# A different beginning: c broadcast by DMA, the first sums on TensorE, and another order of loads and modulation in a two-layer encoder

## The chip, the cores and the metric

The kernel runs on one core of a Trainium2 chip. The metric is the device time of one execution in microseconds, the median of several runs; lower is better. The core has TensorE (PE, with its weight loads listed apart as PEld), VectorE (DVE), ScalarE (ACT), GpSimd (POOL) and SyncE (SP), which issues the transfers between HBM and SBUF. All engines work through queues of their own and wait for one another by semaphores.

## The reference

The reference is an encoder trunk with two layers over 256 tokens of width 2048, in float32. Only the first steps matter for this change; the rest is given in words.

```python
c_act = jax.nn.silu(c)
for l in range(DEPTH):
    mod = c_act @ ada_w[l] + ada_b[l]
    sh_a, sc_a, gt_a, sh_m, sc_m, gt_m = [t[:, None, :] for t in jnp.split(mod, 6, axis=-1)]
    h = rmsnorm(x, norm_mix[l]) * (1.0 + sc_a) + sh_a
    qa, ka, va, qb, kb, vb, ga, gb = split_cols(h @ w_in[l])
    ...  # two attentions, two gates, projections, x = x + gt_a * (merged @ w_out[l])
    h = rmsnorm(x, norm_ffn[l]) * (1.0 + sc_m) + sh_m
    ...  # gated MLP with a convolution over positions, x = x + gt_m * (... @ w_down[l])
```

So the first product `h @ w_in` needs three things: the mean square of each token of x, the shift and scale of each of the 16 chunks of 128 channels (from c and `ada_w`), and the weights.

## The kernel before

**Layout.** Channels lie on the 128 partitions: x is 16 chunks (KC) of 128 channels by 256 tokens. Each weight element is used once for all 256 tokens, so all weights pass through SBUF once, in the order in which they are used.

**Weights.** They come as units of 16 blocks of 128 by 128, one transfer of 1024 KB each (`unit`, L231). ScalarE rounds a unit to a high half (L240), VectorE takes the difference as the low half (L241), and each block then costs three matmuls: high times high, high times low, low times high. In the form `tokens` (L325 to L327), used for q, k and v, four blocks make six matmuls of 512 columns, three for each half of the tokens; in the form `features` (L249 to L251) a block makes three matmuls of 256 columns.

**Modulation.** `ada(l)` makes the 96 columns of shift, scale and gate of a layer. Each column group takes one tile of `ada_w`, 1024 KB, which VectorE multiplies by silu(c) and sums along the free dimension (L172). That wants silu(c) on every partition, in `cact`. The order is shift and scale of chunk 0, then of chunk 1, and so on. Weight tiles and modulation tiles share one pool of four buffers, `raw`.

**The beginning, in program order.** c is loaded as one row of 8 KB (L140); four matmuls with a column of ones copy it to all partitions, and ScalarE applies silu to each quarter (L145, L146). x comes in four transfers of 512 KB (L545). ScalarE squares each quarter of x (L551), VectorE adds the quarters (L553) and folds the four chunks that are left to one (L555), and two matmuls with a column of 1/2048 give each token's mean square (L558, L559). GpSimd raises it to -1/2 (L386), TensorE transposes it to a row (L392), six matmuls on the identity follow as warm-up (L341), and ScalarE copies the row to SBUF (L397). Then h of each chunk is made in three steps: VectorE (L405), ScalarE (L408) and VectorE (L409).

**Parts of q, k and v.** In layer 0 the product with `w_in` is cut along the 16 input chunks into four parts of 2, 4, 5 and 5 chunks (`K_PARTS_0`), so that it can begin before all modulation is there. Each part runs nine column groups of q, k and v and then the 16 groups of gate A over its chunks, and adds to the sums of the parts before (L678 copies in part 0, L680 adds later; L709 and L712 for the gate). A part's blocks make 6.5, 13, 16.25 and 16.25 units.

**Pacing.** `job0` makes modulation and h for one chunk after another. Before part 0 it is run until 4 tiles (2 chunks) are done. It then runs in the background: at the end of each unit `bg.tick()` adds `FIRST_RATE` (0.65) to a count, and for every whole number one tile is made. At the start of a later part, `while done[0] < 2 * (part[-1] + 1)` makes whatever is still missing for that part: 12 tiles in all for part 1, 22 for part 2, 32 for part 3.

**Small tables.** `small(l)` loads the attention mask, the rotary tables, gains, sinks and convolution weights, and forms the rotary tables with gains on VectorE (L572, L577). It is called after the first column group of part 0. Its results are first used in the last part.

**Order.** The framework plans the order of each engine's queue at build time: by the order of the program as priority, and by when it expects an operation's inputs to be there. So an engine's queue can differ from program order, but once built it is worked strictly in its order.

Of the kernel before, what the change touches and what calls it, by code (L numbers as in the profile page):

```python
# [9 lines left out]
F32 = mybir.dt.float32  # L10
F32R = mybir.dt.float32r
AF = mybir.ActivationFunctionType
ALU = mybir.AluOpType
AX = mybir.AxisListType

P = 128
L = 2
D = 2048
S = 256
KC = D // P  # L20
# [6 lines left out]
EPS = 1e-6  # L27
# [18 lines left out]
ADA_PLAN_0 = [(38, 32), (58, 48), (76, 66), (84, 70), (96, 80), (128, 96), (145, 108), (175, 118), (192, 124), (230, 143)]  # L46
ADA_PLAN_1 = [(0, 143), (76, 169), (84, 165), (95, 176), (129, 192)]

FIRST_RATE = 0.65
ENDING = 15  # L50
FIRST = 0

WARM = [1, 4, 3]
WARM_IN = 6
AHEAD = 2
HELD = 2
LATE = 3
# [48 lines left out]
def encoder(ctx: ExitStack, tc: tile.TileContext, a: dict, out: bass.AP):  # L106
    nc = tc.nc
# [3 lines left out]
    def skip(n, p=None):  # L111

        skips.append((p or pool(f"skip{len(skips)}", 1)).tile([P, n // 4], F32, name=f"skip{len(skips)}"))
        nc.vector.memset(skips[-1][:], 0.0)
# [9 lines left out]
    sm = pool("sm", 3)  # L124
    mm = pool("mm", 4, space=bass.MemoryType.PSUM)
    ax = pool("ax", 3, space=bass.MemoryType.PSUM)
# [3 lines left out]
    mean = const.tile([P, 1], F32, name="mean")  # L130
# [6 lines left out]
        return t  # L137

    cact = const.tile([P, D], F32, name="cact")
    nc.sync.dma_start(cact[:1], a["c"])  # L140
    one = sm.tile([1, P], F32, name="one", tag="one", bufs=1)
    nc.vector.memset(one[:], 1.0)
    for i in range(0, D, 512):
        cb = ax.tile([P, 512], F32, name="cb", tag="ax")
        nc.tensor.matmul(cb[:], one[:], cact[:1, i : i + 512], start=True, stop=True)  # L145
        nc.scalar.activation(out=cact[:, i : i + 512], in_=cb[:], func=AF.Silu)  # L146
    x = const.tile([P, KC, S], F32, name="x")
    skip(96, const)
    skip(64)
    sp = pool("s", 1)  # L150

    def place(tag, n, dt, name):
        return sp.tile([P, n, S], dt, name=name, tag=tag)
# [6 lines left out]
    mods, amods, nrms, done = {}, {}, {}, {0: 0, 1: 0}  # L160
# [63 lines left out]
    bg = Paced()  # L224
# [111 lines left out]
    def warm(n):  # L336

        if n:
            ps = ax.tile([P, 512], F32, name="warm", tag="ax")
            for _ in range(n):  # L340
                tc.keep_in_program_order(nc.tensor.matmul(ps[:, :P], ident[:], ident[:], start=True, stop=True))  # L341
# [33 lines left out]
    def normed(l, w, sums, st, first=False):  # L375
# [3 lines left out]
        def steps():  # L379
# [10 lines left out]
            for t in range(2):  # L390
                tc.keep_in_program_order(
                    nc.tensor.transpose(rb[:, t * P : (t + 1) * P], rs[:, t : t + 1].broadcast_to([P, P]), ident[:])  # L392
                )
            warm(WARM_IN if first else WARM[2])
            if first:
# [108 lines left out]
    def urgent(yes):  # L504
        return tc.high_priority() if yes else nullcontext()
# [7 lines left out]
    def ada_all():  # L513
        yield from gens[0]
        yield from gens[1]

    adas = ada_all()
# [14 lines left out]
    def ada_and_h(steps):  # L532

        for kc in range(KC):
            while done[0] < 2 * kc + 1:
                next(adas)
                yield
            next(adas)
            next(steps)
            yield  # L540

    for _ in range(FIRST):
        next(adas)
    for i in range(0, KC, 4):
        nc.sync.dma_start(x[:, i : i + 4], a["xT"][:, i : i + 4])  # L545

    mean_sq = sm.tile([P, 2], F32, name="ms_in", tag="nsa")
    acc = place("y0", 4, F32, "sq_in")
    for i in range(0, KC, 4):
        sq = acc if i == 0 else place(f"y{1 + i // 4 % 2}", 4, F32, f"sq_in{i}")  # L550
        nc.scalar.activation(out=sq[:], in_=x[:, i : i + 4], func=AF.Square)  # L551
        if i:
            nc.vector.tensor_tensor(out=acc[:], in0=acc[:], in1=sq[:], op=ALU.add)  # L553
    for n in (2, 1):
        nc.vector.tensor_tensor(out=acc[:, :n], in0=acc[:, :n], in1=acc[:, n : 2 * n], op=ALU.add)  # L555
    ps = ax.tile([P, 2], F32, name="ss_in", tag="ss", bufs=1)
    for t in range(2):
        nc.tensor.matmul(ps[:, t : t + 1], acc[:, 0, t * P : (t + 1) * P], mean[:], start=True, stop=True)  # L558
    nc.vector.tensor_scalar(out=mean_sq[:], in0=ps[:], scalar1=EPS, scalar2=None, op0=ALU.add)  # L559

    tables = []

    def small(l):

        if l == 0:
            tables.extend((load(a["maskA"], [P, 2, S], "maskA"), load(a["cs"], [P, 2, 2, HALF], "cs")))
        cs = tables[1]
        gains = load(a["gains"][l], [P, 4], f"gains{l}", lay, tag="gains")
        rg = load(a["rg"][l], [P, 2, ROT], f"rg{l}", lay, tag="rg")
        sink = load(a["sink"][l], [P, HA], f"sink{l}", lay, tag="sink")  # L570
        cw = load(a["cw"][l], [P, 2 * FC, 4], f"cw{l}", lay, tag="cw", bufs=1)
        nc.vector.tensor_scalar(out=gains[:, 2:3], in0=gains[:, 2:3], scalar1=SCALE, scalar2=None, op0=ALU.mult)  # L572
        rots = []
        for w in range(2):
            rot = lay.tile([P, 4, 2, HALF], F32, name=f"rot{l}_{w}", tag=f"rot{w}")
            for i, (f, g) in enumerate(((0, 0), (1, 1), (0, 1), (1, 0))):
                nc.vector.tensor_tensor(  # L577
                    out=rot[:, i], in0=cs[:, f],
                    in1=rg[:, w, g * HALF : (g + 1) * HALF].unsqueeze(1).broadcast_to([P, 2, HALF]), op=ALU.mult,
                )  # L580
            rots.append(rot)

        return gains, sink, cw, rots

    for l in range(L):
        st = Stream(l) if l == 0 else nxt
        h, steps = normed(l, 0, None if l == 0 else sums, st, first=l == 0)
        mod = mods.get(l)
        if l == 0:
            job0 = ada_and_h(steps)  # L590
            while done[0] < 2 * len(K_PARTS[0][0]):
                next(job0)
            mod = mods[0]
            bg.add(job0, FIRST_RATE)
        else:
            with urgent(True):
                for _ in range(FEED):
                    next(steps)
            st.steps, st.fed = steps, FEED
# [63 lines left out]
        parts = K_PARTS[l]  # L663
        for pi, part in enumerate(parts):
            if l == 0 and pi > 0:
                while done[0] < 2 * (part[-1] + 1):
                    next(job0)
            last = pi == len(parts) - 1
            for g in range(len(QKV_GROUPS)):
                pss = st.tokens(h, part)  # L670
                if pi == 0 and g == 0:
                    gains, sink, cw, rots = small(l)
                dst = packs[g // 3][:, 4 * (g % 3) : 4 * (g % 3) + 4]
                rows = dst.rearrange("p (t a) s -> p t (a s)", t=2)
                if not last or pi > 0:
                    for t, ps in enumerate(pss):
                        if pi == 0:
                            nc.scalar.copy(rows[:, t], ps[:])  # L678
                        else:
                            nc.vector.tensor_tensor(out=rows[:, t], in0=ps[:], in1=rows[:, t], op=ALU.add)  # L680
                    pss = [rows[:, t] for t in range(2)]
                if not last:
                    continue

                def have(g=g):
                    ready[0] = g + 1

                vcol = {0: GA * HEAD, 4: 0, 7: 0}.get(g)
                if vcol is not None and pi == 0:
                    for t in range(2):  # L690
                        nc.scalar.copy(rows[:, t, vcol:], pss[t][:, vcol:])
                if g == 0:
                    qk_rows(pss, GA, rots[1], gains[:, 1:2], kTa, have)
                elif g < 3:
                    qk_rows(pss, 4, rots[0], gains[:, 0:1], dst, have)
                elif vcol is None:
                    qk_rows(pss, 4, None, gains[:, 3:4] if g in (3, 6) else gains[:, 2:3], dst, have)
                else:
                    have()
                if g == 2:  # L700
                    bg.add(job, ATT[l])


            for mo in range(KC):

                def gate_a(ps):
                    src = ps
                    if pi > 0:
                        nc.vector.tensor_tensor(out=ya[:, mo], in0=ps, in1=ya[:, mo], op=ALU.add)  # L709
                        src = ya[:, mo]  # L710
                    if last:
                        nc.scalar.activation(out=ya[:, mo], in_=src, func=AF.Sigmoid)  # L712
                    elif pi == 0:
                        nc.scalar.copy(ya[:, mo], ps)

                st.features([hs[k] for k in part], [gate_a])
# [11 lines left out]
        for tag in ("y0", "y1", "y2"):  # L728
            t = place(tag, 4, F32, f"gb{l}_{tag}")
            gb += [t[:, i] for i in range(4)]  # L730
        for i in range(2):
            t = ev.tile([P, 2, S], F32, name=f"gb{l}_{i}", tag="u", bufs=2)
# [38 lines left out]
        for mos in OUT_TURNS:  # L771
            end = mos[0] == KC - 1
            if end:
                st.prefetch(AHEAD + 1)
            with urgent(mos[0] >= ENDING):
# [18 lines left out]
        for gi, chunks in enumerate(FF_GROUPS):  # L794
# [48 lines left out]
            for mos in OUT_TURNS:  # L843
                end = mos[0] == KC - 1
                ending = last and mos[0] >= ENDING
                if last and end and l < L - 1:
                    nxt = Stream(l + 1)
                    nxt.prefetch(AHEAD)
                with urgent(ending):
# [76 lines left out]
```

## Time and profile before

| what | value |
|---|---|
| median of 3 runs | 2740.95 us (2740.84 to 2763.34) |
| profiled execution | 2756.37 us |
| its span | 2754.6 us |
| PE busy | 2697.4 us, 98% |
| VectorE busy | 2077.5 us, 75% |
| ScalarE busy | 1371.3 us, 50% |
| read from HBM | 695.03 MB, 253 GB/s over the span |
| modulation tiles, weight units | 192 and 464 transfers of 1024 KB |

How to read it: TensorE's time is nearly the whole span, so an engine's idle time matters only where TensorE waits for it. The profile's slices are 69 us long and coarse; the beginning is read from windows of 2 to 20 us and from the timeline. "PEclk" is the clock that TensorE was granted, as a share of full speed. A matmul's listed duration contains its way through the pipeline, so the pace is read from counts or from the distance between starts, not from durations. A row that ends in "x6" gathers six instructions.

### The profile page before, as it was taken

To read this page: it belongs to the slowest core of one execution; us is meant where nothing else is said; L and a number is where in the kernel's file an instruction comes from. 1 tells how busy PE (TensorE), PEld (TensorE's weight loads), DVE (VectorE), ACT (ScalarE), POOL (GpSimd) and SP (SyncE) were. 2 spreads that over 40 slices of the span, in tenths; PEclk is the share of its full clock that TensorE was granted. 3 is DMA by queue.
4 is the path that set the end of the run, shared out by engine and by line. 5 is a ranking of instruction groups with operands and counts; after the bars stand their busy time and mean duration, and the time that the engine had idled before them with its cause. 6 is when DMAs were issued, how large, how long until landed. Compare 5 with 4: busy or idle time off the path is not lost.

```text
span 2754.6 us, 49972 instructions
## 1 busy us (share of the span) xinstructions
PE 2697.4 (98%) x21136; PEld 2601.5 (94%) x21136; DVE 2077.5 (75%) x2814; ACT 1371.3 (50%) x1897; POOL 39.3 (1%) x24
## 2 busy tenths in 40 slices
PE   7899999999999999999999999999999999999999
PEld 5788799998999999999988889999999999999999
DVE  6998987998887777678877665657888856665664
ACT  5344784444553455345444557544455535544553
POOL 0000100000000000000000000000000000000000
PEclk9999999999999999999999999999999999999999
DMA  8887588986778766677756556665858755555554
GB/s 317 334 333 262 219 303 326 349 337 242 275 283 316 277 248 252 253 277 284 280 197 258 220 211 247 234 249 203 294 221 301 264 192 191 199 192 191 199 188 149
DMA packets 101890, 700.36 MB, mean 254 GB/s; under 512 B 12705, under 2 KB 15009, under 8 KB 17697
## 3 DMA queue, kind: packets, MB, share of 16 engines
q1 hardware_dynamic: 101666, 697.17, 68.5%
q8 instruction: 165, 2.70, 0.4%
q14 instruction: 59, 0.48, 0.0%
HBM read 695.03 MB, written 2.10 MB: 253 GB/s over the span
## 4 chain that ended last, share of the span: by engine, by line
PE 73%; issue 15%; DVE 6%; DMA 2%; ACT 2%; POOL 1%; POOLq 0%; SPq 0%; ACTq 0%; DVEq 0%
PE ps L251 20%; PE ps L249 20%; PE ps L250 20%; PE ps_t L326 4%; PE ps_t L327 4%; PE ps_t L325 4%; DVE hl L241 2%; DVE aw L172 2%; DMA aw<-in_aw 1%; DMA w<-in_ws 1%; POOL qrs L373 1%; ACT hl L240 1%; PE sc L468 1%; PE po L499 1%; DVE qn L432 0%
## 5 line engine op out<-in xcount | busy, mean ns | idle before, releaser
L241 DVE TENSOR_TENSOR hl<-w,hl 128x1024 fp32r<-128x1024 f32 x928 | 1130.6, 1223 | 401.4 <-ACT hl L240 400.0
L240 ACT CAST hl<-w 128x1024 fp32r<-128x1024 f32 x928 | 971.1, 1049 | 850.8 <-PE ps L251 578.9
L249 PE MATMUL ps<-h,hl 128*128 128x256 f32 x3840 | 1073.8, 280 | 3.3 <-ACT hl L240 2.0
L251 PE MATMUL ps<-h,hl 128*128 128x256 f32 x3840 | 1073.6, 280 | 0.0
L250 PE MATMUL ps<-h,hl 128*128 128x256 f32 x3840 | 1072.7, 279 | 0.0
L250 PEld LDWEIGHTS ps<-h,hl 128*128 128x128 f32 x3840 | 728.8, 190 | 0.4
L249 PEld LDWEIGHTS ps<-h,hl 128*128 128x128 f32 x3840 | 723.9, 189 | 4.4 <-ACT hl L240 2.2
L251 PEld LDWEIGHTS ps<-h,hl 128*128 128x128 f32 x3840 | 722.9, 188 | 0.3 <-DVE hl L241 0.2
L172 DVE CUSTOM_DVE_ANT_0 aw<-aw,cact,ab 128x2048 f32<-128x2048 f32 x192 | 450.7, 2347 | 48.5 <-DMA aw<-in_aw 47.7
L790 DVE SCALAR_TENSOR_TENSOR u<-ps,cw,u 128x255 f32<-128x255 f32 x352 | 168.3, 482 | 104.0 <-ACT u L788 97.7
L325 PE MATMUL ps_t<-hl,h 128*128 128x512 f32 x576 | 227.9, 400 | 7.9 <-ACT hl L240 7.2
L326 PE MATMUL ps_t<-hl,h 128*128 128x512 f32 x576 | 228.5, 397 | 4.7 <-DVE hl L241 4.7
L327 PE MATMUL ps_t<-hl,h 128*128 128x512 f32 x576 | 227.5, 396 | 0.9 <-DVE h L409 0.9
L788 ACT ACTIVATE u<-ps,cw 128x256 f32<-128x256 f32 x176 | 98.7, 565 | 247.6 <-PE ps L251 247.6
L250 PE MATMUL ps<-merged,hl 128*128 128x256 f32 x512 | 144.3, 282 | 0.0
L249 PE MATMUL ps<-merged,hl 128*128 128x256 f32 x512 | 143.9, 282 | 0.3 <-DVE m L749 0.3
L251 PE MATMUL ps<-merged,hl 128*128 128x256 f32 x512 | 144.1, 281 | 0.0
L250 PE MATMUL ps<-act_o,hl 128*128 128x256 f32 x512 | 142.9, 279 | 0.0
L251 PE MATMUL ps<-act_o,hl 128*128 128x256 f32 x512 | 142.8, 279 | 0.0
L249 PE MATMUL ps<-act_o,hl 128*128 128x256 f32 x512 | 142.5, 279 | 0.0
L325 PEld LDWEIGHTS ps_t<-hl,h 128*128 128x128 f32 x576 | 109.6, 191 | 31.9 <-ACT hl L240 8.3
L326 PEld LDWEIGHTS ps_t<-hl,h 128*128 128x128 f32 x576 | 109.8, 191 | 30.4 <-DVE hl L241 8.1
(162 smaller groups left out, 3755.8 us busy)
## 6 DMA issues: line engine op xcount, KB each, us to landing
w<-in_ws SPq DMA_DIRECT2D x464, 1024.0 KB, 4.9
aw<-in_aw SPq DMA_DIRECT2D x192, 1024.0 KB, 5.0
bias<-in_bias SPq DMA_DIRECT2D x16, 256.0 KB, 5.1
x<-in_xT SPq DMA_DIRECT2D x4, 512.0 KB, 5.2
out<-x SPq DMA_DIRECT2D x16, 128.0 KB, 2.8
cw<-in_cw SPq DMA_DIRECT2D x2, 176.0 KB, 5.5
maskA<-in_maskA SPq DMA_DIRECT2D x1, 256.0 KB, 5.3
ab<-in_ab SPq DMA_DIRECT2D x2, 48.0 KB, 5.9
```

The costliest lines, as they stand in the source:

```text
L172: nc.vector.tensor_tensor_reduce(out=raw[:], in0=raw[:], in1=cact[:], scale=1.0, scalar=ab[:, i : i + 1], op0=ALU.mult, op1=ALU.add, accum ...
L240: nc.scalar.copy(hl[:, 0], r)
L241: nc.vector.tensor_tensor(out=hl[:, 1], in0=r, in1=hl[:, 0].bitcast(F32), op=ALU.subtract)
L249: nc.tensor.matmul(out, hi, act[:, 0], start=first, stop=False)
L250: nc.tensor.matmul(out, hi, act[:, 1], start=False, stop=False)
L251: nc.tensor.matmul(out, lo, act[:, 0], start=False, stop=last)
L325: nc.tensor.matmul(ps[:], xh, hi, start=kc == kcs[0], stop=False)
L326: nc.tensor.matmul(ps[:], xh, lo, start=False, stop=False)
L327: nc.tensor.matmul(ps[:], xl, hi, start=False, stop=kc == kcs[-1])
L373: nc.gpsimd.tensor_tensor(out=dst, in0=src, in1=mhalf[:, :k], op=ALU.pow)
L788: nc.scalar.activation(out=u, in_=ps, func=AF.Identity, scale=w[:, 1:2], bias=w[:, 3:4])
L790: nc.vector.scalar_tensor_tensor(out=u[:, to], in0=ps[:, of], scalar=w[:, j : j + 1], in1=u[:, to], op0=ALU.mult, op1=ALU.add)
```

## The change

Five edits, all in the beginning.

1. c is loaded straight to all 128 partitions by one transfer from a repeated row; the column of ones and its four matmuls go. Silu runs on two halves in SBUF. The transfers of x are issued right behind it.
2. The sums of squares: the quarters of x are squared by ScalarE and VectorE in turn, and TensorE sums all 16 chunks directly, with 32 one-column matmuls into two accumulators, kept in program order. VectorE adds epsilon to each. Fourteen warm-up matmuls follow.
3. `st.prefetch(1)` asks for the first weight unit after two modulation tiles, no longer after four.
4. The rate of `job0` is 1.25 tiles a unit in part 0, 0.8 in part 1 and 0.65 after that, no longer 0.65 throughout.
5. `small(l)` is called in the last part but one (part 2 in layer 0; in layer 1, which has one part, nothing changes).

```diff
-FIRST_RATE = 0.65
+FIRST_RATE = [1.25, 0.8, 0.65]
...
-FIRST = 0
...
+WARM_FIRST = 14
...
     cact = const.tile([P, D], F32, name="cact")
-    nc.sync.dma_start(cact[:1], a["c"])
-    one = sm.tile([1, P], F32, name="one", tag="one", bufs=1)
-    nc.vector.memset(one[:], 1.0)
-    for i in range(0, D, 512):
-        cb = ax.tile([P, 512], F32, name="cb", tag="ax")
-        nc.tensor.matmul(cb[:], one[:], cact[:1, i : i + 512], start=True, stop=True)
-        nc.scalar.activation(out=cact[:, i : i + 512], in_=cb[:], func=AF.Silu)
     x = const.tile([P, KC, S], F32, name="x")
+    nc.sync.dma_start(cact[:], a["c"].broadcast_to([P, D]))
+    for i in range(0, KC, 4):
+        nc.sync.dma_start(x[:, i : i + 4], a["xT"][:, i : i + 4])
+    for i in range(0, D, D // 2):
+        nc.scalar.activation(out=cact[:, i : i + D // 2], in_=cact[:, i : i + D // 2], func=AF.Silu)
...
-    acc = place("y0", 4, F32, "sq_in")
-    for i in range(0, KC, 4):
-        sq = acc if i == 0 else place(f"y{1 + i // 4 % 2}", 4, F32, f"sq_in{i}")
-        nc.scalar.activation(out=sq[:], in_=x[:, i : i + 4], func=AF.Square)
-        if i:
-            nc.vector.tensor_tensor(out=acc[:], in0=acc[:], in1=sq[:], op=ALU.add)
-    for n in (2, 1):
-        nc.vector.tensor_tensor(out=acc[:, :n], in0=acc[:, :n], in1=acc[:, n : 2 * n], op=ALU.add)
-    ps = ax.tile([P, 2], F32, name="ss_in", tag="ss", bufs=1)
+    ps = [ax.tile([P, 512], F32, name=f"ss_in{t}", tag="ax") for t in range(2)]
+    for i in range(0, KC, 4):
+        sq = place(f"y{i // 4 % 3}", 4, F32, f"sq_in{i}")
+        if i // 4 % 2:
+            nc.vector.tensor_tensor(out=sq[:], in0=x[:, i : i + 4], in1=x[:, i : i + 4], op=ALU.mult)
+        else:
+            nc.scalar.activation(out=sq[:], in_=x[:, i : i + 4], func=AF.Square)
+        for k in range(4):
+            for t in range(2):
+                tc.keep_in_program_order(
+                    nc.tensor.matmul(
+                        ps[t][:, :1], sq[:, k, t * P : (t + 1) * P], mean[:], start=i + k == 0, stop=i + k == KC - 1
+                    )
+                )
     for t in range(2):
-        nc.tensor.matmul(ps[:, t : t + 1], acc[:, 0, t * P : (t + 1) * P], mean[:], start=True, stop=True)
-    nc.vector.tensor_scalar(out=mean_sq[:], in0=ps[:], scalar1=EPS, scalar2=None, op0=ALU.add)
+        nc.vector.tensor_scalar(out=mean_sq[:, t : t + 1], in0=ps[t][:, :1], scalar1=EPS, scalar2=None, op0=ALU.add)
+    warm(WARM_FIRST)
...
             job0 = ada_and_h(steps)
+            while done[0] < 2:
+                next(job0)
+            st.prefetch(1)
             while done[0] < 2 * len(K_PARTS[0][0]):
                 next(job0)
             mod = mods[0]
-            bg.add(job0, FIRST_RATE)
+            bg.add(job0, FIRST_RATE[0])
...
                 while done[0] < 2 * (part[-1] + 1):
                     next(job0)
+                bg.pace(job0, FIRST_RATE[min(pi, len(FIRST_RATE) - 1)])
...
-                if pi == 0 and g == 0:
+                if pi == max(0, len(parts) - 2) and g == 0:
                     gains, sink, cw, rots = small(l)
```

More of the change, by code (lines that the diff above doesn't have):

```diff
@@ L540, in ada_and_h @@
             yield
-    for _ in range(FIRST):
-        next(adas)
+    mean_sq = sm.tile([P, 2], F32, name="ms_in", tag="nsa")
+    ps = [ax.tile([P, 512], F32, name=f"ss_in{t}", tag="ax") for t in range(2)]
     for i in range(0, KC, 4):
-        nc.sync.dma_start(x[:, i : i + 4], a["xT"][:, i : i + 4])
-    mean_sq = sm.tile([P, 2], F32, name="ms_in", tag="nsa")
-    acc = place("y0", 4, F32, "sq_in")
-    for i in range(0, KC, 4):
-        sq = acc if i == 0 else place(f"y{1 + i // 4 % 2}", 4, F32, f"sq_in{i}")
-        nc.scalar.activation(out=sq[:], in_=x[:, i : i + 4], func=AF.Square)
-        if i:
-            nc.vector.tensor_tensor(out=acc[:], in0=acc[:], in1=sq[:], op=ALU.add)
-    for n in (2, 1):
-        nc.vector.tensor_tensor(out=acc[:, :n], in0=acc[:, :n], in1=acc[:, n : 2 * n], op=ALU.add)
-    ps = ax.tile([P, 2], F32, name="ss_in", tag="ss", bufs=1)
+        sq = place(f"y{i // 4 % 3}", 4, F32, f"sq_in{i}")
[10 more added lines that the diff above has]
+                )
     for t in range(2):
-        nc.tensor.matmul(ps[:, t : t + 1], acc[:, 0, t * P : (t + 1) * P], mean[:], start=True, stop=True)
-    nc.vector.tensor_scalar(out=mean_sq[:], in0=ps[:], scalar1=EPS, scalar2=None, op0=ALU.add)
+        nc.vector.tensor_scalar(out=mean_sq[:, t : t + 1], in0=ps[t][:, :1], scalar1=EPS, scalar2=None, op0=ALU.add)
+    warm(WARM_FIRST)
     tables = []
```

## The prediction

> **What bounds the kernel now.** I read the page from the top: busy times, then the slices of the span.
>
> ```profile
> span 2754.6 us, 49972 instructions
> PE 2697.4 (98%) x21136; PEld 2601.5 (94%) x21136; DVE 2077.5 (75%) x2814; ACT 1371.3 (50%) x1897; POOL 39.3 (1%) x24
> ...
> PE   7899999999999999999999999999999999999999
> ...
> PEclk9999999999999999999999999999999999999999
> DMA  8887588986778766677756556665858755555554
> ```
>
> TensorE is busy 98% of the span, so what can be won is its idle time (57 us in all) and time at a lowered clock. The two slices below 9 are the first two, 69 us each, which is where the change works. Next I cut the beginning into windows; each row gives the stretch and its length, busy time (and instruction count) of PE, PEld, DVE, ACT, POOL, then granted clock, DMA share and GB/s.
>
> ```profile
> 0.00:10.00 10.00, 7.32 (x8) 2.32 (x8) 0.77 (x7) 6.14 (x7) 0.70 (x6) 1.00 0.80 283
> 10.00:20.00 10.00, 1.22 (x5) 0.93 (x4) 8.82 (x10) 2.49 (x3) 0.00 (x0) 1.00 0.97 395
> 20.00:30.00 10.00, 5.25 (x18) 4.25 (x19) 8.22 (x13) 3.26 (x5) 2.87 (x1) 1.00 0.99 370
> 30.00:40.00 10.00, 10.00 (x35) 7.97 (x35) 6.17 (x14) 4.95 (x8) 0.00 (x0) 1.00 0.55 202
> 40.00:60.00 20.00, 20.00 (x102) 16.59 (x101) 14.35 (x15) 15.86 (x26) 0.00 (x0) 1.00 0.82 310
> 60.00:80.00 20.00, 11.52 (x82) 9.85 (x81) 19.03 (x22) 8.84 (x20) 0.00 (x0) 0.81 0.97 353
> ...
> 100.00:120.00 20.00, 20.00 (x90) 16.54 (x90) 19.95 (x24) 9.16 (x10) 0.00 (x0) 1.00 0.89 334
> ...
> 200.00:240.00 40.00, 40.00 (x280) 37.40 (x279) 35.59 (x48) 16.25 (x17) 0.00 (x0) 1.00 0.85 311
> ...
> 440.00:480.00 40.00, 40.00 (x355) 40.00 (x354) 33.18 (x32) 15.63 (x21) 0.00 (x0) 1.00 0.93 347
> ```
>
> Three things stand here. From 10 to 30 us the DMA engines are full and TensorE does little: data is late. From 30 to 60 us the DMA share falls to 0.55 and 0.82 and VectorE is idle 3.8 + 5.65 = 9.5 us. From 60 to 80 us VectorE and DMA are full again while TensorE stands still 8.5 us. Work that could have been done between 30 and 60 is done too late. The counts also give the pace: 0.222 us for a 512-column matmul (100 to 120 us) and 0.113 us for a 256-column one (40 us / 355).
>
> The timeline shows what the stall is: a row is start, duration, engine, line, tile and, in brackets, the wait.
>
> ```profile
> 55.16 14.15 SPq L171 DMA_DIRECT2D aw<-in_aw  x6
> ...
> 64.14 2.35 DVE L172 CUSTOM_DVE_ANT_0 aw<-aw,cact,ab 128x2048 f32<-128x2048 f32 x1
> ...
> 78.18 2.35 DVE L172 CUSTOM_DVE_ANT_0 aw<-aw,cact,ab 128x2048 f32<-128x2048 f32 x1
> ...
> 79.79 1.22 PE L325 MATMUL ps_t<-hl,h 128*128 128x512 f32 x2 [6.89 <-ACT hl L240]
> 82.12 0.80 PE L326 MATMUL ps_t<-hl,h 128*128 128x512 f32 x1 [1.11 <-DVE hl L241]
> ```
> ```profile
> 74.00:76.00 2.00, 0.00 (x0) 0.00 (x0) 2.00 (x4) 0.00 (x0) 0.00 (x0) 0.50 1.08 385
> ...
> 84.00:86.00 2.00, 2.00 (x6) 1.62 (x5) 1.96 (x3) 1.08 (x2) 0.00 (x0) 0.50 0.93 303
> 86.00:88.00 2.00, 2.00 (x9) 1.58 (x9) 1.57 (x5) 1.00 (x2) 0.00 (x0) 0.95 0.96 406
> ```
>
> This is the border between part 0 (chunks 0 and 1) and part 1 (chunks 2 to 5). Part 0 is 104 blocks, 6.5 units of 16, and six units end in it. At 0.65 a unit that makes 3 modulation tiles on top of the first 4, so 12 - 7 = 5 are fetched and reduced at once. Some ten 512-column matmuls of part 1 get through before TensorE waits. It runs steadily from 82.1, and the clock is 0.50 until about 86, costing 2 us. Part 1 starts in effect at 82.1 - 10 x 0.222 + 2 = 81.9 us. That is the number to beat.
>
> **The change part by part.** First the prices: the beginning, then rows of the page.
>
> ```profile
> 2.63 7.58 PE L145 MATMUL cb<-cact,one 1*128 1x512 f32 x8 [2.63 <-DMA cact<-in_c]
> ...
> 9.54 1.23 DVE L553 TENSOR_TENSOR sq_in<-sq_in,sq_in 128x1024 f32<-128x1024 f32 x1 [8.41 <-ACT sq_in L551]
> ...
> 10.73 1.99 ACT L551 ACTIVATE sq_in<-x 128x1024 f32<-128x1024 f32 x2
> ...
> 17.75 0.93 PEld L558 LDWEIGHTS ss_in<-mean,sq_in 128*128 128x128 f32 x4 [9.13 <-DVE sq_in L555]
> ...
> 17.76 0.43 SPq L136 DMA_DIRECT2D maskA<-in_maskA  x1
> ...
> 20.13 2.87 POOL L386 TENSOR_TENSOR nrs<-ms_in,mhalf 128x2 f32<-128x2 f32 x1 [18.82 <-DVE ms_in L559]
> ...
> 20.37 0.43 SPq L136 DMA_DIRECT2D cw<-in_cw  x1
> ...
> 23.32 2.68 PEld L341 LDWEIGHTS warm<-ident 128*128 128x128 f32 x12
> ...
> 28.98 0.48 DVE L409 SCALAR_TENSOR_TENSOR h<-ht,mod,h 128x256 fp32r<-128x256 f32 x1
> 29.11 0.79 PE L326 MATMUL ps_t<-hl,h 128*128 128x512 f32 x1 [1.70 <-DVE hl L241]
> ...
> 30.64 0.90 DVE L577 TENSOR_TENSOR rot<-cs,rg 128x32 f32<-128x32 f32 x8
> ```
> ```profile
> L241 DVE TENSOR_TENSOR hl<-w,hl 128x1024 fp32r<-128x1024 f32 x928 | 1130.6, 1223 | 401.4 <-ACT hl L240 400.0
> ...
> L172 DVE CUSTOM_DVE_ANT_0 aw<-aw,cact,ab 128x2048 f32<-128x2048 f32 x192 | 450.7, 2347 | 48.5 <-DMA aw<-in_aw 47.7
> ...
> w<-in_ws SPq DMA_DIRECT2D x464, 1024.0 KB, 4.9
> aw<-in_aw SPq DMA_DIRECT2D x192, 1024.0 KB, 5.0
> ...
> maskA<-in_maskA SPq DMA_DIRECT2D x1, 256.0 KB, 5.3
> ```
>
> *c by DMA.* Gone are eight matmul passes (7.6 us) that lay beside the loading of x; they cost nothing. Added is a transfer that writes 128 rows of 8 KB, 1024 KB, ahead of x on a full queue: at 395 GB/s 1.049 MB is 2.65 us. No row shows a transfer that reads one row 128 times. Between nothing (if the repeated row is cheap) and twice that (5.3 us, if it is dear) I take 2.65, the price of the 1024 KB tiles nearest to it.
>
> *Weights sooner, small tables later.* Before, what must land for the first unit is x (2.1 MB), four modulation tiles and w0: 7.3 MB. After, the order is c, x, aw0, aw1, w0, aw2, aw3. The rows move 2.83 + 3.95 + 3.70 MB in the first 30 us, so 6.3 MB (w0) are through at 18.8 and 8.4 MB (aw3) at 24.3. There are four buffers, so aw3 is asked for only when aw0 has been reduced, around 16 to 17 us; that is in time. About 1 us of completion, 2.35 for its reduction and 1.4 for h of chunk 1 give 29.1; before, that h is written at 28.98 + 0.48. So chunk 0's six matmuls come earlier, chunk 1's do not: 0 to 2 us won.
>
> *Sums on TensorE.* VectorE loses three adds of 1.23 and two small ones and gets two products and two small ones: 2.2 us less. TensorE gets 16 x 2 matmuls, each two passes as in the row of ss_in (4 records for 2): 64 passes. At 0.93 us for four overlapping loads, and 2.68 for twelve, a pass takes 0.21 to 0.22 us, so 13.7 us; at double clock half of that. They start after both halves of silu and the first square, near 9.6, and end between 16.6 and 23.3. The end was 18.8 before. Fourteen warm-up matmuls (28 passes, 3 to 6 us) follow, beside the 2.87 us on GpSimd, and the transposes of the scale queue behind them. At half clock h of chunk 0 comes at about 31.4, at full clock the weights of 18.8 us set it.
> The cb row bears on which clock: eight passes of 512 columns in 7.6 us, with one row in use, hold the same 0.85 us a pass from first to last. The Trainium skill (TensorE: Matmul & The Clock Gate, Part 1: The HAM clock gate) says that some 3.4 us of sustained activity release the full clock; the cb row does not agree for thin matmuls. By the page the sums would take about 9 us and end near 18.5, by the row 13.7 us and 23.3.
>
> *More modulation in part 0.* At 1.25 a unit six units make 7 tiles, and one is left for the border instead of five. Each unit then needs 2.25 MB blocks. At 353 to 395 GB/s that is 6.0 to 6.7 us, against 34.8 / 6.5 = 5.35 us of matmuls (108 x 0.222 + 96 x 0.113 = 34.8 us for the part). VectorE needs 2 x 1.14 + 1.25 x 2.35 + 0.6 for h = 5.8 us. So part 0 becomes bound by the loads, lightly, with about 0.8 us of idle TensorE per unit.
> The Trainium skill (DMA: Bandwidth & Descriptors, Specifications) puts the limit of one core's HBM reads at about 358 GB/s, which gives 6.6 us a unit; the row of 10 to 20 us here shows 395, so I do not hold to it.
>
> When does part 1 start? Three bounds. **Loads:** c, x, 12 modulation tiles and 7 units are 22 blocks, 23.1 MB; 10.5 are in by 30 us, 12.6 follow at 353 to 395 GB/s until 62 to 66, then two splits (2.35) and the last half unit (24 x 0.113 = 2.7): 67 to 71. **VectorE:** 57.4 us busy by 80 us, 59.4 by 82; minus 2.2 and the 1.05 of the tables 56.1, of which 2.5 lie before aw0 is in at 14.5: 68 with no gap, 70 with a gap such as now. **TensorE:** 29.1 - 1.4 + 34.8 + 2 (half clock) = 64.5. I take 70: **12 us won**.
>
> *Part 1.* Its 13 units take 216 x 0.222 + 192 x 0.113 = 69.6 us of matmuls, and VectorE is at 19.95 of 20 there. The faster rate, 0.8, moves one or two reductions out of the next border into a full VectorE: nothing won, nothing lost.
>
> *Part 2, the tables.* Six loads (0.43 us of SP each, 2.6) leave the queue between w0 and w1 and stand in part 2's. VectorE's nine small products (1.05 us) go with them; if they reach the head of its queue before the tables land, up to 5.3 us more. Everything queued behind them is splits and reductions. The 200 to 240 row has 4.4 us of idle VectorE to absorb it. Between 0 and 6 I take 1, and 1 more for the one tile left at the first border.
>
> **Sum:** 12 - 2 = 10 us. The profiled execution took 2756.37 us (span 2754.6), 15 above the median, so 2746 there; from the median of 2740.95, **2731 us**, 0.4% less. TensorE is the bound for the rest, and its order of work there is unchanged, so the gain is not given back.
>
> **The rivals.**
> *The sums hold VectorE.* If they run at half clock until 23.3 and the two small additions stand in VectorE's queue ahead of a reduction, VectorE idles from 19.3 (behind aw1) or 14.5 (ahead of aw0) until then: 4 to 9 us off a gain of 10, some 3 us left, 2738. For it: the cb row, and VectorE works its queue in order. Against: the clock may rise.
> *TensorE's clock stays halved through part 0 (the slower side).* The windows show the clock at 0.50 after some us of waiting. If every unit's wait is long enough to bring that, part 0's matmuls take 2 x 34.8 = 69.6 us and end at 98.7, 17 us later than now: 2758. It decides where a unit takes over about 8 us, loads below 295 GB/s. Against: 353 and more in the full stretches, and 0.8 us of idle a unit where the stall that dropped the clock was several.
> *Loads and VectorE overlap better than I allow.* Then TensorE's own 64.5 holds, 17 us won: 2724.
> *The order written is not the order issued.* A planner orders the queues; if it pulls the tables or the splits elsewhere and the border stall stays, the time is that of now, 2741.
>
> **How the numbers follow.** Forecast (2726 to 2735) 0.48; held VectorE 0.25; better overlap 0.13; same order as now 0.07; halved clock 0.05; something not seen 0.02. The range 2718 to 2747 takes in 7 us around the end cases for the scatter of runs and leaves out the halved clock. One per cent, 27 us, is about what a measurement can tell here; all my named cases lie within it, so faster 0.03, same 0.93, slower 0.04.
>
> **What would show it.** Right: no stall of TensorE above 3 us between the first steady matmul and 100 us, DMA share above 0.9 from 30 to 60 us, VectorE full there, part 1 steady at about 70, and the same distance as now from there to the end. Half-clock sums: the last ss_in pass at 23, VectorE idle before ms_in. It would be wrong if c's transfer takes much more than 3 us, if rot waits on its tables in part 2, or if the steady stages after 250 us change length.

## The result

The changed kernel is slower: 2763.12 us median against 2746.19, a ratio of 1.0057 with a 95% interval of 1.0029 to 1.0085. The ratio is that of the means over the runs that lie within 1.5% of each kernel's fastest. The forecast was 2731 us, a gain of 0.4%. One thing comes first, since it decides how the rest is read: single executions of one kernel lie up to 60 us apart (2728 to 2788 for the kernel before), and the traces show where. Here are two long stages of the same kernel before in two profiled executions; the columns are those of the windows, for TensorE alone (stretch, length, busy time and count of matmuls, granted clock, DMA share, GB/s).

```profile
1000.00:1040.00 40.00, 40.00 (x342) 1.00 0.66 242
2300.00:2340.00 40.00, 40.00 (x355) 1.00 0.55 197
```
```profile
1000.00:1040.00 40.00, 40.00 (x356) 1.00 0.67 250
2300.00:2340.00 40.00, 40.00 (x342) 1.00 0.51 185
```

With no idle time and a granted clock of 1.00 in both, TensorE completes 342 or 355 (356) matmuls in 40 us: two paces, 0.117 and 0.113 us a matmul. The MLP of each layer runs in one or the other for nearly all of its length. Over some 650 us of a layer that is, as an estimate, 24 us, more than the whole beginning could give. So beside the ratios I compare the traces up to a landmark ahead of those stages: the moment at which VectorE begins to split unit 7, the first unit that lies wholly in part 1 (units are counted from 0), and the same for unit 37, just behind the start of part 3.

The page of the changed kernel shows nothing bad. TensorE's second slice has even gone from 8 to 9.

```profile
span 2762.1 us, 50120 instructions
PE 2708.2 (98%) x21216; PEld 2615.5 (95%) x21216; DVE 2077.0 (75%) x2811; ACT 1368.5 (50%) x1892; POOL 39.3 (1%) x24
...
PE   7999999999999999999999999999999999999999
...
PEclk9999999999999999999999999999999999999999
DMA  8887578997778766677757656665758755555554
```

The second slice is fuller because the stall at the border is smaller: from unit 6's split to unit 7's are 9.9 us (76.8 to 86.7), 19.6 before (61.2 to 80.8). The first slice hides the loss, since 64 one-column passes and 28 warm-up passes count as work there. The windows show it (busy time and count of PE, PEld, DVE, ACT and POOL, then granted clock, DMA share, GB/s).

```profile
10.00:20.00 10.00, 10.00 (x48) 10.00 (x49) 1.22 (x1) 0.81 (x1) 0.00 (x0) 1.00 1.02 421
20.00:30.00 10.00, 9.74 (x55) 9.55 (x55) 5.69 (x9) 1.00 (x3) 2.83 (x1) 1.00 0.39 145
30.00:40.00 10.00, 4.25 (x14) 2.88 (x15) 9.48 (x10) 3.21 (x4) 0.00 (x0) 0.87 0.77 301
40.00:60.00 20.00, 20.00 (x79) 15.76 (x78) 16.69 (x21) 12.90 (x21) 0.00 (x0) 0.89 0.90 342
60.00:80.00 20.00, 17.42 (x112) 15.19 (x112) 15.43 (x16) 13.83 (x27) 0.00 (x0) 0.91 0.85 330
```

From 10 to 20 us VectorE (third pair) works 1.22 us where it worked 8.82 before. From 20 to 30 the DMA share is 0.39 where it was 0.99: six microseconds of loading are lost. The clock column is no guide in the first rows: it reads 1.00 from 10 to 20 us, while in the prewarmed run below passes just as far apart stand under 0.50. So I read the clock from the distance between passes: 0.214 us up to 27.2 us, 0.112 behind that. I call the first half clock. The same holds for the prediction's rows ahead of 30 us. The timeline of the changed kernel says why the loads stopped.

```profile
8.44 19.49 SPq L169 DMA_DIRECT2D aw<-in_aw  x3
...
8.92 13.82 PE L552 MATMUL ss_in<-mean,sq_in 128*128 128x1 f32 x64 [8.92 <-ACT sq_in L548]
...
22.35 0.16 DVE L557 TENSOR_SCALAR ms_in<-ss_in 128x1 f32<-128x1 f32 x1 [8.53 <-PE ss_in L552]
...
22.60 5.58 PE L339 MATMUL warm<-ident 128*128 128x128 f32 x28
...
22.94 2.35 DVE L170 CUSTOM_DVE_ANT_0 aw<-aw,cact,ab 128x2048 f32<-128x2048 f32 x1
23.02 2.83 POOL L384 TENSOR_TENSOR nrs<-ms_in,mhalf 128x2 f32<-128x2 f32 x1 [21.72 <-DVE ms_in L557]
...
28.02 0.38 PE L390 MATMUL rb<-ident,nrs 128*128 128x128 f32 x2
```

The sums run from 8.92 to 22.74 us at 0.214 us a pass. The small addition behind them (L557) stands ahead of the first reduction in VectorE's queue and holds it for 8.53 us. All four buffers are full meanwhile, so SP can issue no further load: its three modulation loads stretch over 19.49 us. The scale then waits for the warm-up as well: GpSimd is done at 25.85, the transposes start at 28.0. The landmark, unit 7's split, in the kernel before and in the changed one:

```profile
80.85 2.35 DVE L241 TENSOR_TENSOR hl<-w,hl 128x1024 fp32r<-128x1024 f32 x2
```
```profile
86.74 2.36 DVE L239 TENSOR_TENSOR hl<-w,hl 128x1024 fp32r<-128x1024 f32 x2 [0.45 <-ACT hl L238]
```

It is 5.9 us late. The loads lost 6.0 from 20 to 30 us (10 x (0.99 - 0.39)), but they win part of that back from 30 to 60, so that the two agree is no proof. At unit 37 it is 251.0 against 243.3, 7.7 late. Both profiled executions have the slow pace at 1000 us and the fast one at 2300 (342 and 355 in both), so their spans can be compared: they differ by 7.5. The distance of the medians, 17 us, is more than that. The lowest runs of each, 2729.4 and 2738.6, are 9 us apart.

### The profile page after: what moved, and what is told of

It reads as the page before. It is cut to its first block, busy times and chain, and to the rows that moved or that the text cites. A ratio compares the mean times of both kernels' runs of the same rounds, so it can differ in the third digit from the quotient of the medians.

```text
span 2762.1 us, 50120 instructions
## 1 busy us (share of the span) xinstructions
PE 2708.2 (98%) x21216; PEld 2615.5 (95%) x21216; DVE 2077.0 (75%) x2811; ACT 1368.5 (50%) x1892; POOL 39.3 (1%) x24
## 4 chain that ended last, share of the span: by engine, by line
PE 77%; issue 14%; DVE 5%; ACT 2%; POOL 1%; DMA 1%; POOLq 0%; DVEq 0%; ACTq 0%
PE ps L249 21%; PE ps L248 21%; PE ps L247 21%; PE ps_t L324 4%; PE ps_t L325 4%; PE ps_t L323 4%; DVE hl L239 2%; DVE aw L170 1%; ACT hl L238 1%; POOL qrs L371 1%; PE ss_in L552 1%; PE sc L466 0%; DMA aw<-in_aw 0%; PE po L497 0%; PE warm L339 0%
```

## The experiments

**Old sums in the changed kernel.** My theory after the result: the sums hold the beginning. The rival: the pace of 1.25 starves TensorE.

```diff
-    ps = [ax.tile([P, 512], F32, name=f"ss_in{t}", tag="ax") for t in range(2)]
...  # 32 one-column matmuls, warm(WARM_FIRST)
+    acc = place("y0", 4, F32, "sq_in")
...  # the adds and folds of the kernel before
```

> The changed kernel with its sums of squares made as before (three adds and two folds on VectorE, two matmuls, no warm-up of 14). Theory 1, the sums at half clock hold the beginning: the scale is there at about 20 us instead of 28.4, h of chunk 1 at about 30 instead of 39, part 1 steady about 9 us sooner than in the changed kernel; the kernel comes out 3 to 8 us faster than the one before (ratio 0.997 to 0.999). Theory 2, the faster pace starves TensorE in part 0: the kernel stays 4 to 8 us slower than before (ratio 1.0015 to 1.003).

Measured: ratio 0.9978 (0.9932 to 1.0024) to the kernel before, which leaves the sign open. In its trace the first step of h is at 20.97, the loads keep running (20 to 30 us), and unit 7 is split at 78.0.

```profile
15.88 0.16 DVE L553 TENSOR_SCALAR ms_in<-ss_in 128x2 f32<-128x2 f32 x1 [1.11 <-PE ss_in L552]
16.04 2.35 DVE L170 CUSTOM_DVE_ANT_0 aw<-aw,cact,ab 128x2048 f32<-128x2048 f32 x1
...
20.97 0.48 DVE L403 SCALAR_TENSOR_TENSOR ht<-x,amod,rbs 128x256 f32<-128x256 f32 x1
```
```profile
20.00:30.00 10.00, 7.55 (x23) 5.38 (x22) 8.80 (x12) 2.51 (x4) 0.00 (x0) 1.00 0.94 345
30.00:40.00 10.00, 8.82 (x32) 6.97 (x33) 8.43 (x12) 6.70 (x11) 0.00 (x0) 0.83 0.98 351
40.00:60.00 20.00, 17.77 (x74) 13.89 (x74) 18.22 (x20) 12.22 (x19) 0.00 (x0) 0.91 0.97 350
60.00:80.00 20.00, 15.07 (x105) 13.30 (x104) 15.21 (x16) 12.20 (x25) 0.00 (x0) 0.97 0.87 335
```
```profile
78.03 2.36 DVE L239 TENSOR_TENSOR hl<-w,hl 128x1024 fp32r<-128x1024 f32 x2 [0.45 <-ACT hl L238]
```

The sums with their warm-up cost 8.7 us at unit 7 (86.7 against 78.0) and 9.3 at unit 37 (251.0 against 241.7). Without them the change is 2.8 us ahead of the kernel before at unit 7 and 1.6 at unit 37, not the 12 and 10 that I had forecast (and a second profile of the kernel before, below, takes even this lead away). So the sums explain why it is slower, but not why the rest won so little.

**Old pace in the changed kernel.**

```diff
-FIRST_RATE = [1.25, 0.8, 0.65]
+FIRST_RATE = [0.65, 0.65, 0.65]
```

> The changed kernel with the pace of modulation back at 0.65 throughout. Theory 1 (sums): the beginning stays late by 3 us at the first unit and 9 at the second, and the burst of five tiles at the border of parts 0 and 1 is back, so it is the slowest of all: 10 to 15 us slower than before (ratio 1.004 to 1.006). Theory 2 (pace): it loses its handicap and is within 4 us of the kernel before (ratio 1.000 to 1.0015).

Measured: ratio 1.0016 (0.9979 to 1.0054); unit 7 at 84.8, unit 37 at 250.0. Against the kernel before that is 3.9 and 6.7 us late, at the rival's limit of 4 and beyond it. Against the changed kernel it is 2.0 and 1.0 us ahead. So the pace is not the handicap, and the burst that is back costs nothing that can be seen: my own 10 to 15 us do not show either. Within what one profile can tell, the pace is worth nothing here.

**The new sums alone in the kernel before.**

```diff
-    acc = place("y0", 4, F32, "sq_in")
...
+    ps = [ax.tile([P, 512], F32, name=f"ss_in{t}", tag="ax") for t in range(2)]
...  # 32 one-column matmuls, then warm(14)
```

> The kernel before with the sums on TensorE and the warm-up of 14 alone. Theory 1: 64 passes at 0.21 us end near 22, VectorE stands before its first reduction from about 12 to 22 us, and the kernel is 6 to 12 us slower than before (ratio 1.002 to 1.0045). Theory 2: same as before within 2 us, or 2 us faster from the adds taken off VectorE and the clock that is up at the first unit.

Measured: ratio 1.0027 (0.9979 to 1.0075). The trace is clearer than the ratio: the additions end at 24.0, and unit 7 is split at 90.56, unit 37 at 253.9.

```profile
23.43 0.16 DVE L564 TENSOR_SCALAR ms_in<-ss_in 128x1 f32<-128x1 f32 x1 [8.53 <-PE ss_in L559]
...
90.56 2.35 DVE L242 TENSOR_TENSOR hl<-w,hl 128x1024 fp32r<-128x1024 f32 x2
```

That is 9.7 and 10.6 us after the kernel before, as the theory of the sums has it.

**The addition moved off VectorE.** Is it the place in VectorE's queue, or the whole chain?

```diff
-        nc.vector.tensor_scalar(out=mean_sq[:, t : t + 1], in0=ps[t][:, :1], scalar1=EPS, ...)
+        nc.scalar.activation(out=mean_sq[:, t : t + 1], in_=ps[t][:, :1], func=AF.Identity, bias=eps[:])
...  # eps: a column filled with EPS
```

> The changed kernel with the addition of epsilon on ScalarE instead of VectorE; nothing else differs. If the two additions at the head of VectorE's queue are what costs (a queue order that can be mended), the first reductions start at 14 instead of 23 us and the kernel gains 6 to 9 us on the changed one. If the chain of the sums itself costs (sums to 22.7, warm-up to 28.2, then the scale), VectorE only stands one place later, before the first h, until 28.4: the gain on the changed kernel is 0 to 2 us.

Measured: ratio 1.0039 (0.9997 to 1.0081); unit 7 at 86.4.

```profile
13.98 2.35 DVE L172 CUSTOM_DVE_ANT_0 aw<-aw,cact,ab 128x2048 f32<-128x2048 f32 x1
16.32 2.35 DVE L172 CUSTOM_DVE_ANT_0 aw<-aw,cact,ab 128x2048 f32<-128x2048 f32 x1
...
29.68 0.48 DVE L405 SCALAR_TENSOR_TENSOR ht<-x,amod,rbs 128x256 f32<-128x256 f32 x1 [10.80 <-ACT rbs L397]
```

The first reductions start 9 us sooner, and VectorE then stands 10.80 us before the first h, which wants the scale. The wait has only moved one place down the queue: the chain of sums, warm-up and scale is the cause, not the addition.

**TensorE warmed before the sums.**

```diff
+    pw = ax.tile([P, 512], F32, name="prewarm", tag="ax")
+    for _ in range(18):
+        tc.keep_in_program_order(nc.tensor.matmul(pw[:, :P], ident[:], ident[:], start=True, stop=True))
```

> The changed kernel with 18 extra matmuls of 128 columns on the identity ahead of the sums, while TensorE waits for c and x (36 passes of 0.21 us, from about 1.5 to 9 us). If the sums are slow only because TensorE begins them cold, they run at 0.11 us a pass, end near 17 instead of 22.7, VectorE's first reduction starts near 17 instead of 22.9 and unit 7 is split 5 to 6 us sooner than in the changed kernel. If one-column passes do not keep the clock up, the clock falls back during the sums, which then end at 20 to 23, and unit 7 comes 0 to 2 us sooner.

```profile
1.36 7.10 PE L545 MATMUL prewarm<-ident 128*128 128x128 f32 x36 [1.36 <-POOL ident masks.py:199]
...
8.76 12.08 PE L555 MATMUL ss_in<-mean,sq_in 128*128 128x1 f32 x64 [0.30 <-ACT sq_in L551]
```

The 36 passes take 7.10 us, less than the 7.7 of a half clock throughout, so the clock rose near their end. The 64 passes behind them still take 12.08 us, 1.7 less than without. Two windows of this run show it, for TensorE alone (stretch, length, busy time and count, granted clock, DMA share, GB/s):

```profile
8.80:10.60 1.80, 1.80 (x17) 1.00 1.05 388
12.60:20.00 7.40, 7.40 (x36) 0.50 1.00 420
```

About 17 passes ran fast, and then the clock fell. One-column passes did not keep it up, as the second theory had it. Unit 7 is split at 84.3, 2.5 us sooner than in the changed kernel, which is within the scatter of one profile (below).

**No warm-up behind the sums.**

```diff
-WARM_FIRST = 14
+WARM_FIRST = 0
```

> The changed kernel without the 14 warm-up matmuls behind the sums. Theory 1, they only delay: the transposes of the scale start when GpSimd is done, near 25.9 instead of 27.9, and the first h comes with the end of the second reduction, 1 us sooner; unit 7 about 1 us sooner. Rival, they raise the clock for the first units: TensorE is at half clock from 30 us on, the first unit takes 2 to 3 us longer, and unit 7 is the same or 1 to 2 us later.

Measured: the transposes start at 26.02, 2.0 sooner; the first unit then runs at half clock until 33.6; unit 7 is split at 84.65, 2.1 us sooner, and unit 37 at 248.1, 2.9 sooner. Both effects are there. That the delay is the larger is likely but not shown: 2 to 3 us are within the scatter of one profile.

**The old way of c beside the old sums.**

```diff
-    nc.sync.dma_start(cact[:], a["c"].broadcast_to([P, D]))
+    nc.sync.dma_start(cact[:1], a["c"])
...  # four matmuls with a column of ones, silu on quarters
```

> The changed kernel with the old sums and the old way of c (one row, copied by matmul). If the broadcast costs what 1024 KB cost in a full queue, x and everything behind it comes 2.65 us sooner than with the old sums alone: unit 7 at about 75.5 against 78.0 there and 80.8 in the kernel before, and 4 us ahead of the kernel before at the end of part 2. If the loads are not what sets part 0, unit 7 stays near 78.

Measured: unit 7 at 79.4, unit 37 at 243.4, both later by 1.4 to 1.7 us than with the broadcast. The 1024 KB did not cost their 2.65 us at the landmark. Why it is not sooner is not settled: the first splits are at 23.1 and 23.0, and from 20 to 30 us the loads move 282 GB/s, where they moved 345 with the broadcast.

**The kernel before, once more.**

> The kernel before once more, for the scatter of one execution. Theory: the scatter of the total (2728 to 2788) comes from the two paces of the matmuls seen in the long stages (342 or 355 in 40 us), and the beginning repeats: unit 7 is split at 80.8 within 0.5 us. If the beginning itself scatters, unit 7 moves by several us and no difference of a few us in the beginning can be trusted from one profile.

```profile
78.25 2.35 DVE L241 TENSOR_TENSOR hl<-w,hl 128x1024 fp32r<-128x1024 f32 x2
```

Measured: unit 7 is split 2.6 us sooner than in the other profile, and unit 37 1.6 sooner, not within the expected 0.5. So one profile can place a landmark only to 2 or 3 us. The 8 to 10 us of the sums stand clear of that, and both ways: the sums taken out of the changed kernel, and put into the kernel before. The leads of 2 to 4 us in the variants do not; against this profile the old sums lead by 0.2 us at unit 7 and by nothing at unit 37.

**Why the rest won nothing.** Four kernels on the old sums. The first two change the pace:

```diff
-FIRST_RATE = [1.25, 0.8, 0.65]
+FIRST_RATE = [0.65, 0.65, 0.65]   # and, in the other, [1.34, 0.8, 0.65]
```

> The changed kernel with the old sums and the old pace of 0.65: only c by DMA, weights sooner and the tables later are left of the change. If the pace is worth nothing because the same tiles must pass before unit 7 either way, unit 7 is split within 1.5 us of 78.0 (old sums alone) and part 0 ends sooner (unit 6 near 60 instead of 68) with a stall of 15 us or more behind it. If the pace is what brought the old-sums kernel its lead, unit 7 is at 81 or later.

> The kernel with the old sums and a pace of 1.34 in part 0, so that six units make all eight tiles and no tile is left at the border. If the last tile at the border is what is late, unit 7 is split 2 us or more before 78.0. If only the sum of tiles and units counts, it stays within 1 us of 78.0.

Measured, on the changed kernel with the old sums: at 0.65 unit 6 is split at 57.2 and unit 7 at 77.2; at 1.34 unit 6 at 74.2 and unit 7 at 76.5 and 78.1 (its halves; one tile fewer is reduced ahead of it); at 1.25 they were 68.1 and 78.0. The stall of 20 us behind unit 6 is only handed out among the units before it. The other two make the modulation of tiles 4 to 12 cheaper; they leave out half of the products of those nine tiles, so they compute something else and serve for the time alone:

```diff
+            m = D // 2 if l == 0 and 4 <= n < 13 else D
...  # the reduction over [:, :m] alone; in the second kernel the load too
```

> The kernel with the old sums; for modulation tiles 4 to 12 of layer 0 VectorE reduces only the first half of each tile (the loads stay whole), so that part of the computation is left out. If VectorE sets the pace of part 0, nine reductions of 2.35 us become 1.2 and unit 7 is split 8 to 10 us sooner, near 69. If the loads set it, unit 7 gains 0 to 3 us.

> As the one with half the reductions, but the loads of those nine tiles are halved too (512 KB each), so half of their products are left out of the sums. If the loads set the pace, 4.7 MB less at 0.35 MB/us bring unit 7 some 10 us sooner than with half the reductions alone. If VectorE sets it, the two are within 2 us of each other.

Half the reductions alone, then half the loads too:

```profile
75.91 2.36 DVE L240 TENSOR_TENSOR hl<-w,hl 128x1024 fp32r<-128x1024 f32 x2
```
```profile
68.44 1.23 DVE L240 TENSOR_TENSOR hl<-w,hl 128x1024 fp32r<-128x1024 f32 x1 [0.45 <-ACT hl L239]
```

Ten microseconds less of VectorE bring 2.1 us; 4.7 MB less of loads bring 7.5 more, of the 13 that they take at 0.35 MB a microsecond. So the loads set part 0 in the main, whatever the pace. Half the loads with whole reductions were not run, so how much of the 7.5 needs the cheaper reductions too stays open.

None of these is a version that clearly beats both kernels: the leads at unit 37 are under 2 us where nothing is left out.

## Why the prediction was wrong

**The sums on TensorE: the mechanism was on the list, the weight was not.** The step gave 13.7 us, an end at 23.3 and h of chunk 0 at 31.4; measured were 13.82, 22.74 and 29.91. I kept the full-clock case as the likelier and put the held VectorE at 0.25, though the only row with thin matmuls spoke for it. By an estimate from the Trainium skill (TensorE: Matmul & The Clock Gate, Part 1: The HAM clock gate) they would have ended near 18.5; they ran 13.8 us without a pause and stayed at half clock, so the trace does not agree with it for one-column passes, and the prewarmed run shows the clock falling during them.

**The price of that rival** was 4 to 9 us; it measured 8.7 at unit 7, with the warm-up behind the sums (2.1 less in the run without it, which is within the scatter). But I took it off a gain of 10 that was not there, and so ended at 2738 where the sign should have turned.

**The gain of 12 us at the border is the step that failed.** It had three bounds for part 1, the loads at 67 to 71. Loads were in the main the right bound, as the halved loads show; their term was mis-sized twice. First, I counted 22 blocks, to the end of part 0. What part 1 runs on is unit 7, and SP's queue has w6, aw11, aw12 and w7 in that order: 24 blocks. The kernel before needs 23 ahead of the same unit, so the change saves no block there at all. With the old sums the first 22 have landed at 66.3 (aw11), the late end of the forecast's 62 to 66, and w7 lands at 73.0, 6.7 us behind them. With that the late end of the forecast's bound, 71, becomes 77.7; unit 7 was split at 78.0. Second, and smaller, I let the loads run at 353 to 395 GB/s without a break. With the old sums they run at 345 to 351 from 20 to 60 us, and their share falls to 0.87 from 60 to 80 us, since SP waits for VectorE to free a buffer (one row of the waits of SP's queue with the old sums, up to 82 us: total, times, longest):

```profile
SPq L169 <- DVE hl L239: 19.8, 5, 5.9
```

The longest of these ends at 65.1, behind the split of unit 5, and from 64 to 66 us the DMA share is 0.43. VectorE also has the last word: w7 lands 5.0 us before its split, and in between VectorE has most of two reductions and the last h to do. With half the reductions w7 lands at 74.4 and is split 1.5 us later, so there the loads hold again.

The limit of about 358 GB/s in the Trainium skill (DMA: Bandwidth & Descriptors, Specifications), to which the forecast did not hold, agrees with these later stretches better than the 395 of 10 to 20 us did.

What remained was the idle share of 30 to 60 us (0.55 and 0.82 before, 0.98 and 0.97 with the old sums): 10 x 0.43 + 20 x 0.15 = 7.3 us, of which the 1024 KB of c take up to 2.65, and 2.8 were measured against the first profile of the kernel before, 0.2 against the second.

**Pace.** "More modulation in part 0" was right that six units would become load-bound; it called this light. In the changed kernel the first and second unit are split 10.2 us apart (30.8 and 41.1), later ones up to 8.6 (62.7 and 71.4), and the clock dropped in these two gaps, as the rival of the halved clock had it, though not for the whole part. The first drop is in the rows of 30 to 60 us above (0.87 and 0.89); this is the second:

```profile
64.00:68.00 4.00, 4.00 (x14) 3.15 (x13) 3.93 (x5) 0.59 (x1) 0.00 (x0) 0.60 0.92 356
```

**c, the weights, the tables.** The quarters of x landed 2.0 to 2.1 us later (the first at 7.1 against 5.1), a little less than the 2.65 priced; the first square, at 7.83 against 5.12, also waited for silu on ScalarE. Chunk 1's h came 3.8 us later with the old sums (32.8 against 29.0) where level was forecast: VectorE split the first unit ahead of the reductions of aw2 and aw3, which ended at 29.9 (26.9 before), and reduced aw4 ahead of the last step of that h. The 1 us of completion in that sum has no row of its own. From unit 7 to unit 37 the changed kernel loses 1.8 us more; I had 1 for the tables, between 0 and 6. That the gain "is not given back" could not be tested, as there was none.

**The total.** About 8 of the 17 us between the medians are shown in the beginning. The rest is within the size of the two paces, and it stays open whether the change makes the slower one more frequent or the runs fell so: in the traces either pace is found in either layer, of the kernel before and of variants of the changed one. The 17 us themselves are not firm: over the 35 runs beside the first experiments the kernel before has a median of 2755.97, 10 us above that of the 20 runs in the result.

## What to carry to other kernels

When background work is asked for sooner, count the blocks that pass the shared buffers before the first consumer that was late, in the old order and in the new: if the count is the same, the stall is moved and not removed. A sum handed to an idle engine is judged by when its result is there, and by who stands behind that result in a queue; here three adds and two folds on VectorE were 8.7 us cheaper than 64 thin passes on TensorE with their warm-up. Where totals scatter by more than the change can give, compare landmarks in the traces, and take a second profile of the same kernel to see how well they repeat.

## What the hardware showed

Two steady paces of TensorE, 342 and 355 matmuls of 256 columns in 40 us, both at a granted clock of 1.00 and without idle time; mostly a whole MLP stage runs at one of them, by estimate 24 us apart over a layer. What chooses is not shown. Here 64 one-column fp32 passes in a row stayed 0.214 us apart for 13.8 us, and behind a raised clock they let it fall within some 2 us (8.8 to 10.7 us in the prewarmed run), while passes of 128 columns raised it after 4.6 us (22.6 to 27.2 in the changed kernel). The granted clock reads 1.00 in the first 27 us of the changed kernel's trace, whatever the passes show. A transfer that reads one 8 KB row 128 times lands as the other loads of 1024 KB do (last column, us from issue to landing):

```profile
w<-in_ws SPq DMA_DIRECT2D x464, 1024.0 KB, 4.9
...
cact<-in_c SPq DMA_DIRECT2D x1, 1024.0 KB, 5.2
```
